# Halved operands for the low-rank products, head sums and centering of a time-mixing layer

## The chip, the cores and the metric

The kernel runs on one core of a Trainium2 chip. The metric is the device time of one execution in microseconds. Times of several runs are given as their median. The profile is of one execution of its own.

## What is computed

One inference step of a two-layer decoder trunk, a prompt of 512 tokens and 8 sample sequences of 8 tokens sharing the weights (576 columns in the kernel). Layer 0 mixes over time (RWKV-7), layer 1 uses windowed attention; each layer has two gated feed-forward blocks. Only the mixing of layer 0 is touched by the change:

```python
w_log = -softplus(-(w0 + tanh(xw @ w1) @ w2)) - 0.5
decay = exp(-exp(w_log))
a = sigmoid(a0 + (xa @ a1) @ a2)            # low rank, 64
g = sigmoid(xg @ g1) @ g2                   # low rank, 160
kk = k * k_k;  kk = kk / max(sqrt(sum(kk*kk, per head)), 1e-12)
k = k * (1 + (a - 1) * k_a);  b = kk * a
# per token: S = S*w + (S @ -kk) b^T + v k^T;  y = S r
y = (y - mean(y, per head)) * rsqrt(var + eps) * lnx_w + lnx_b
y = y + sum(r * k * r_k, per head) * v
return (y * g) @ w_o
```

## The kernel before

Everything is kept with features on the partitions: 1024 features are 8 tiles of 128, and one such tile, two heads, is called a pair (p = 0 to 7). A product over the 576 columns is made in two halves of 288 (`halves`).

**Dense products.** The large weights come in fp32 and are split: `load_w` (line 166) loads 512 columns on SP's queue, ACT copies them to a rounded type (`H`, line 177) and POOL subtracts to get the rest (`L`, line 178). The activations are split the same way by `split` (line 160). A product then is three passes, `WH XH + WH XL + WL XH` (line 697). Smaller products, among them the ones of the change, are plain fp32 matmuls.

**The stage.** The phase "r" (line 1719) loads constants (`rwkv_consts`, line 1678): `bo` sums over the 64 rows of a head, `cen` subtracts the mean of a head. `rwkv` (line 631) makes the mixed inputs, the low-rank activations `tw`, `ta` (rows 0 to 63 for the rate a, rows 64 to 95 for the last 32 rows of the gate) and `sg` (lines 653 to 670). Then it weaves five streams of work (line 823):

- `keys` and `inverses` for each pair: decay, normalised key (`kk`, line 864, with a head sum on line 868), rate a (line 881), the scaled keys B and K (lines 914 to 917), and the inverse of a small triangular matrix on DVE with two trips through DRAM (lines 948 to 962). The keys of pair p wait for the chain of pair p-4.
- `scores` for each pair, after the chain of pair p-2: products between keys and queries, a Neumann series, then the bonus sum (line 1068, whose input `y` is written on line 1063 into one of two buffers, so the post step of pair p-2 has to be through), transposes.
- `chain` for each pair, one after the other: 8 chunks, each a short round of PE and DVE.
- `decode` and `post` for each pair: the centering (line 1197), the variance (line 1207), the gate (lines 1220 and 1221) and a split of the result. The last pair has its own version, `post_last`.
- the dense products: key, receptance and value projections, then the output projection in parts.

**Order.** `weave` (line 578) is a planner: it runs the streams against a clock of its own, which each product advances by its expected length (line 567), always takes the stream that is ready first, and lets the dense stream in at a limited rate, more when few columns were planned lately. A stream's `yield 0.9` is a pause of 0.9 us on that clock, in which other streams' work is placed. A scheduler below it orders each engine's instructions by this sequence and by when buffers come free. Each engine then executes its queue in order.

Of the kernel before, what the change touches and what calls it, by code (L numbers as in the profile page):

```python
# [9 lines left out]
F32R = mybir.dt.float32r  # L10
# [45 lines left out]
N_P = 5  # L56
# [36 lines left out]
class Body:  # L93
# [537 lines left out]
    def rwkv(self, done, wi):  # L631
        nc, I, O = self.nc, self.I, self.O
# [7 lines left out]
        for k in range(DT):  # L640
            n = self.ht(k, "n")
            nc.vector.scalar_tensor_tensor(n, self.h[k], self.vec("n01", k), rs, op0=ALU.mult, op1=ALU.mult)
            x = self.ht(k, "h")
# [9 lines left out]
        tw = self.s("tw")  # L653
# [9 lines left out]
        self.dense(I["w1"], K8, xm, lambda hf, ps, sl: self.act(tw[0:64, sl], ps, AF.Tanh), nw=64, outer=True)  # L663
        ta = self.s("ta")
        self.dense(I["a1"], K8, self.mixed("ma", "AR", M_A), lambda hf, ps, sl: nc.scalar.copy(ta[0:64, sl], ps), nw=64, outer=True)
        sg = self.s("sg")
        xg = self.mixed("mg", "AR", M_A)
        self.dense(I["g1a"], K8, xg, lambda hf, ps, sl: self.act(sg[:, sl], ps, AF.Sigmoid), outer=True)
        self.dense(I["g1b"], K8, xg, lambda hf, ps, sl: self.act(ta[64:96, sl], ps, AF.Sigmoid), nw=32, outer=True)
        self.tw, self.ta, self.sg = tw, ta, sg  # L670

# [151 lines left out]
        self.weave([chain_gen(), score_gen(), rest_gen(), key_gen(), dense_gen(seq)], R_LS, R_RATE, R_WARM)  # L823

    def keys(self, p, V):

        nc, I, c_ = self.nc, self.I, self.rc
# [3 lines left out]
        A, R = V["AR"][:, 0], V["AR"][:, 1]  # L831
# [10 lines left out]
        lw2 = self.s("l1", cols=128)[0:65]  # L842
        la2 = self.s("l2", cols=128)[0:64]
        for t, n in ((lw2, "w2"), (la2, "a2")):
            nc.sync.dma_start(t, I[n][p])
        st = self.s("p1", N_P, cols=512)
# [17 lines left out]
        kk = self.s("p1", N_P)  # L864
        nc.scalar.activation(kk, k, AF.Square, scale=self.vec("kk", p))
        for sl in halves:
            ps = self.bank("w", HF)
            self.mm(ps, c_["bo"], kk[:, sl], start=True, stop=True)
            nc.vector.tensor_scalar(kk[:, sl], ps, 1e-24, None, op0=ALU.max)
            yield 0.9  # L870
            self.mark(f"kk{p}")
# [6 lines left out]
        a = self.s("p1", N_P)  # L878
        for sl in halves:
            ps = self.bank("w", HF)  # L880
            self.mm(ps, la2, self.ta[0:64, sl], start=True, stop=True)
            self.act(a[:, sl], ps, AF.Exp, scale=-1.0, bias=self.na0[:, p:p + 1])
            yield 0.9
            self.mark(f"a{p}")
# [87 lines left out]
    def scores(self, p, V):  # L972
# [91 lines left out]
        bkc = BK[:, 0:NC].rearrange("p c z t -> p c (z t)")  # L1064
        nc.vector.tensor_tensor(bkc, bkc, V["pcc"].to_broadcast([128, NC, 128]), op=ALU.mult)
        for sl in halves:
            ps = self.bank("i", HF)
            self.mm(ps, c_["bo"], y[:, sl], start=True, stop=True)
            nc.vector.tensor_tensor(v[:, sl], ps, v[:, sl], op=ALU.mult)
            yield 0.5  # L1070
            self.mark(f"neu{p}")
# [113 lines left out]
    def post(self, p, V, z):  # L1185
# [3 lines left out]
        self.mark(f"post{p}")  # L1189
        lg2 = self.s("l3", cols=128)  # L1190
        lg3 = self.s("l4", cols=128)
        for t, n in ((lg2, "g2a"), (lg3[64:96], "g2b")):
            nc.sync.dma_start(t, I[n][p])
        yc, s2 = V["y"], V["s2"]
        for sl in halves:
            ps = self.bank("q", HF)
            self.mm(ps, c_["cen"], yc[:, sl], start=True, stop=True)
            nc.scalar.copy(yc[:, sl], ps)
            yield 0.8
            self.mark(f"post{p}")  # L1200
# [17 lines left out]
        for sl in halves:  # L1218
            ps = self.bank("q", HF)
            self.mm(ps, lg2, self.sg[:, sl], start=True, stop=False)  # L1220
            self.mm(ps, lg3[64:96], self.ta[64:96, sl], start=False, stop=True)
            nc.vector.tensor_tensor(zt[:, sl], ps, yc[:, sl], op=ALU.mult)
            yield 0.8
            self.mark(f"post{p}")
# [4 lines left out]
    def post_last(self, p, V, z):  # L1229
# [3 lines left out]
        self.mark(f"post{p}")  # L1233
        lg2 = self.s("l3", cols=128)
        lg3 = self.s("l4", cols=128)
        for t, n in ((lg2, "g2a"), (lg3[64:96], "g2b")):
            nc.sync.dma_start(t, I[n][p])
        yc, rd, bv = V["y"], V["s2"], V["bv"]
        gt, gw = self.s("vo", N_VO), self.s("vo", N_VO)
        for sl in halves:  # L1240
            ps = self.bank("q", HF)
            self.mm(ps, lg2, self.sg[:, sl], start=True, stop=False)
            self.mm(ps, lg3[64:96], self.ta[64:96, sl], start=False, stop=True)
            nc.scalar.copy(gt[:, sl], ps)
            nc.gpsimd.tensor_scalar(gw[:, sl], gt[:, sl], self.vec("lw", p), None, op0=ALU.mult)
            nc.vector.scalar_tensor_tensor(gt[:, sl], bv[:, sl], self.vec("lb", p), gt[:, sl], op0=ALU.add, op1=ALU.mult)
            yield 0.8
            self.mark(f"post{p}")
# [429 lines left out]
    def rwkv_consts(self):  # L1678
        nc = self.nc
        self.rc = {}  # L1680
        for n in ("tri", "triS", "bo", "cen", "id", "bm", "mb", "md", "mq"):
            self.rc[n] = self.const(n, self.ph)
        self.leps = self.ph.tile([128, 1], F32, name="leps")
        nc.vector.memset(self.leps, LNX_EPS)
# [173 lines left out]
```

## Time and profile before

| | us |
|---|---|
| median of 3 runs (2851.83 to 2859.78) | 2859.17 |
| the profiled execution, its own time | 2855.7 |
| its span, first to last instruction | 2853.9 |

Busy shares of the span: PE 95% (2723.6 us), its weight loads 89%, DVE 55%, POOL 54%, ACT 45%. The mean granted clock of TensorE is 0.981 of full speed.

How to read the profile: PE is the matrix engine (PEld its weight loads, which run beside it), DVE the vector engine, ACT the scalar engine, POOL the general one, SP the queue that issues loads. `ps_w<-p,bo` is a product into the PSUM tile ps_w from the tiles p and bo. An fp32 product stands as two records. The records' ends are modelled, so what a product holds PE for is read from one start to the next. A name such as `p` or `l` stands for all tiles of that name with a number behind it.

### The profile page before, as it was taken

To read this page: it belongs to the slowest core of one execution; us is meant where nothing else is said; L and a number is where in the kernel's file an instruction comes from. 1 tells how busy PE (TensorE), PEld (TensorE's weight loads), DVE (VectorE), ACT (ScalarE), POOL (GpSimd) and SP (SyncE) were. 2 spreads that over 40 slices of the span, in tenths; PEclk is the share of its full clock that TensorE was granted. 3 is DMA by queue.
4 is the path that set the end of the run, shared out by engine and by line. 5 is a ranking of instruction groups with operands and counts; after the bars stand their busy time and mean duration, and the time that the engine had idled before them with its cause. 6 is when DMAs were issued, how large, how long until landed. Compare 5 with 4: busy or idle time off the path is not lost.

```text
span 2853.9 us, 56130 instructions
## 1 busy us (share of the span) xinstructions
PE 2723.6 (95%) x21952; PEld 2540.3 (89%) x21952; DVE 1560.1 (55%) x3258; ACT 1297.2 (45%) x2548; POOL 1528.6 (54%) x1256
## 2 busy tenths in 40 slices
PE   8999997998999999999999999999999999999997
PEld 7999996986767778999999999999888878999997
DVE  6543529557677756633436554243577776533435
ACT  4443535434333225434545444353555655443544
POOL 5665748554243335756753466574544325766753
PEclk9999998999999999999999999999999999999999
DMA  4232234222112112232333222324334443232323
GB/s 134 83 96 85 85 97 151 67 69 57 53 40 80 41 47 84 78 97 86 98 92 103 93 82 93 91 80 125 108 85 104 141 141 115 79 92 86 93 86 96
DMA packets 177085, 257.80 MB, mean 90 GB/s; under 512 B 46889, under 2 KB 70897, under 8 KB 176820
## 3 DMA queue, kind: packets, MB, share of 16 engines
q1 hardware_dynamic: 148736, 223.56, 26.1%
q10 hardware_dynamic: 28084, 30.66, 4.1%
q8 instruction: 172, 2.82, 0.4%
q14 instruction: 93, 0.76, 0.1%
HBM read 234.31 MB, written 19.85 MB: 89 GB/s over the span
## 4 chain that ended last, share of the span: by engine, by line
PE 51%; DVE 6%; ACT 2%; issue 1%; DMA 1%; POOL 0%; DVEq 0%; ACTq 0%; POOLq 0%
PE ps_e L204 23%; PE ps_e L409 15%; PE ps_d L561 5%; PE ps_d L409 2%; PE ps_s L561 2%; PE ps_o L561 1%; DVE S L1357 1%; PE ps_pt L570 1%; DVE ps_q L351 1%; DVE S L1352 1%; DMA D<-rev 1%; DVE x L321 0%; ACT sh L343 0%; ACT QS L1426 0%; ACT wh L177 0%
## 5 line engine op out<-in xcount | busy, mean ns | idle before, releaser
L178 POOL TENSOR_TENSOR wl<-wr,wh 128x512 fp32r<-128x512 f32 (+2 forms) x477 | 604.9, 1277 | 728.1 <-ACT wh L177 687.8
L204 PE MATMUL ps_e<-hv,wh 128*128 128x288 f32 x2944 | 588.6, 295 | 2.5 <-POOL hv L163 1.3
L177 ACT CAST wh<-wr 128x512 fp32r<-128x512 f32 (+2 forms) x477 | 277.2, 587 | 546.4 <-PE ps_e L204 293.2
L204 PEld LDWEIGHTS ps_e<-hv,wh 128*128 128x128 f32 x2944 | 473.4, 188 | 3.8 <-POOL hv L163 2.2
L204 PE MATMUL ps_e<-hv,wl 128*128 128x288 f32 x1472 | 434.8, 296 | 1.2 <-POOL wl L178 1.2
L561 PE MATMUL ps_d<-x,wh 128*128 128x288 f32 x1664 | 369.1, 309 | 6.2 <-ACT wh L177 2.2
L204 PE MATMUL ps_e<-x,wh 128*128 128x288 f32 x1792 | 362.6, 297 | 10.6 <-ACT x L269 7.4
L204 PEld LDWEIGHTS ps_e<-x,wh 128*128 128x128 f32 x1792 | 289.5, 189 | 12.6 <-ACT x L269 7.4
L561 PEld LDWEIGHTS ps_d<-x,wh 128*128 128x128 f32 x1664 | 274.4, 191 | 26.6 <-issue 9.3
L204 PEld LDWEIGHTS ps_e<-hv,wl 128*128 128x128 f32 x1472 | 276.9, 188 | 1.5 <-POOL wl L178 1.4
L466 DVE SCALAR_TENSOR_TENSOR h<-ps_e,h 128x288 f32<-128x288 f32 x192 | 87.7, 457 | 335.0 <-PE ps_e L204 335.0
L204 PE MATMUL ps_e<-x,wl 128*128 128x288 f32 x896 | 264.5, 296 | 0.0
L561 PE MATMUL ps_d<-x,wl 128*128 128x288 f32 x832 | 250.2, 301 | 0.3 <-POOL wl L178 0.3
L409 PE MATMUL ps_e<-x,wh 128*128 128x288 f32 x1056 | 213.2, 295 | 0.0
L346 POOL TENSOR_TENSOR wl<-wr,wh 128x512 fp32r<-128x512 f32 x136 | 197.2, 1454 | 18.3 <-ACT wh L343 12.6
L409 PE MATMUL ps_e<-TH,wh 128*128 128x288 f32 x544 | 163.3, 300 | 9.8 <-DVE t L383 6.9
L409 PEld LDWEIGHTS ps_e<-x,wh 128*128 128x128 f32 x1056 | 169.1, 188 | 3.9 <-issue 3.9
L204 PEld LDWEIGHTS ps_e<-x,wl 128*128 128x128 f32 x896 | 169.0, 189 | 0.2
L409 PE MATMUL ps_e<-TH,wl 128*128 128x288 f32 x544 | 161.4, 297 | 0.0
L561 PEld LDWEIGHTS ps_d<-x,wl 128*128 128x128 f32 x832 | 159.1, 191 | 2.2 <-issue 0.5
L409 PE MATMUL ps_e<-TL,wh 128*128 128x288 f32 x544 | 160.9, 296 | 0.0
L409 PE MATMUL ps_e<-x,wl 128*128 128x288 f32 x528 | 155.1, 295 | 0.0
(402 smaller groups left out, 6395.4 us busy)
## 6 DMA issues: line engine op xcount, KB each, us to landing
wr<-in_f1wi SPq DMA_DIRECT2D x108, 256.0 KB
wr<-in_f2wi SPq DMA_DIRECT2D x108, 256.0 KB
sr<-in_f1wi SPq DMA_DIRECT2D x68, 256.0 KB
sr<-in_f2wi SPq DMA_DIRECT2D x68, 256.0 KB
wr<-in_f1wo SPq DMA_DIRECT2D x64, 256.0 KB
wr<-in_f2wo SPq DMA_DIRECT2D x64, 256.0 KB
wr<-in_wrkv SPq DMA_DIRECT2D x48, 256.0 KB
wr<-in_wq SPq DMA_DIRECT2D x48, 256.0 KB
```

Source lines behind the costliest of these rows:

```text
L177: nc.scalar.copy(H, raw)
L178: nc.gpsimd.tensor_tensor(L, raw, H.bitcast(F32), op=ALU.subtract)
L204: nc.tensor.matmul(ps[0:nw], a, b[:, sl], start=k + m == 0, stop=3 * k + m == n - 1)
L346: eng.tensor_tensor(L, a, H.bitcast(F32), op=ALU.subtract)
L351: i = nc.vector.tensor_tensor(t, a, b, op=op).ins
L409: nc.tensor.matmul(ps, a, b, start=first and k + m == 0, stop=k == DT // 2 - 1 and m == 2, skip_group_check=True)
L466: nc.vector.scalar_tensor_tensor(h[:, sl], ps, 0.5, h[:, sl], op0=ALU.mult, op1=ALU.add)
L561: self.nc.tensor.matmul(out, lhsT, rhs, **kw)
L570: self.nc.tensor.transpose(out, in_, ident)
L1352: nc.vector.tensor_tensor_reduce(dst, ps, bias, -1.0, 3.0e38 if mx is None else mx, op0=ALU.add, op1=ALU.min, accum_out=m)
L1357: nc.vector.tensor_tensor(S[:, a], S[:, a], S[:, b], op=ALU.add)
```

## The change

The head sums of the squared key (line 868) and of the bonus product (line 1068) and the centering (line 1197, pairs 0 to 6) no longer use fp32 operands. Their moving operand is split into two rounded halves (`halves_of`: ACT copies, POOL subtracts, two buffers H shared by the three users), and the product is two passes against a rounded constant (`mm2`). The rate product (line 881) and the two gate products (lines 1220, 1221 and in `post_last`) are made of three passes (`mm3`); their weights are split after loading (`small`, ACT and POOL), and `ta` and `sg` are split once, ahead of the pairs. The first three get a pause of 2.5 us in the planner after the split. The centering of the last pair, the variance sums and the decay products stay fp32. In `rwkv`, `ta` and `sg` now lie in the ring `p1` until they are split into tiles of their own.

```diff
@@ rwkv
-        ta = self.s("ta")
+        ta = self.s("p1", N_P)
...
-        sg = self.s("sg")
+        sg = self.s("p1", N_P)
...
-        self.tw, self.ta, self.sg = tw, ta, sg
+        self.tw = tw
+        self.ta, self.sg = self.dbl("taR", 1, F32R), self.dbl("sgR", 1, F32R)
+        for a, b in ((slice(0, 64), nc.vector), (slice(64, 96), nc.gpsimd)):
+            self.split(ta[a], self.ta[a, 0], self.ta[a, 1], b)
+        self.split(sg, self.sg[:, 0], self.sg[:, 1])
@@ new functions
+    def small(self, ap, tag, rows):
+        t = self.s(tag, cols=128)
+        HL = self.ph.tile([128, 2, 128], F32R, name=tag + "R", tag=tag + "R", bufs=1)
+        self.nc.sync.dma_start(t[rows], ap)
+        return self.split(t[rows], HL[rows, 0], HL[rows, 1], self.nc.gpsimd)
+
+    def mm3(self, ps, W, X, sl, rows=slice(0, 128), first=True, last=True):
+        (WH, WL), (XH, XL) = W, (X[rows, 0, sl], X[rows, 1, sl])
+        for m, (a, b) in enumerate(((WH, XH), (WH, XL), (WL, XH))):
+            self.mm(ps, a, b, start=first and m == 0, stop=last and m == 2)
+
+    def mm2(self, ps, c, X, sl):
+        for i in range(2):
+            self.mm(ps, c, X[i][:, sl], start=i == 0, stop=i == 1)
+
+    def halves_of(self, x):
+        return self.split(x, self.s("H", 2, F32R), self.s("H", 2, F32R), self.nc.gpsimd)
@@ keys
-        la2 = self.s("l2", cols=128)[0:64]
+        la2 = self.small(I["a2"][p], "l2", slice(0, 64))
...
+        sq = self.halves_of(kk)
+        yield 2.5
...
-            self.mm(ps, c_["bo"], kk[:, sl], start=True, stop=True)
+            self.mm2(ps, self.boR, sq, sl)
...
-            self.mm(ps, la2, self.ta[0:64, sl], start=True, stop=True)
+            self.mm3(ps, la2, self.ta, sl, slice(0, 64))
@@ scores
+        yR = self.halves_of(y)
+        yield 2.5
...
-            self.mm(ps, c_["bo"], y[:, sl], start=True, stop=True)
+            self.mm2(ps, self.boR, yR, sl)
@@ post
-        lg2 = self.s("l3", cols=128)
-        lg3 = self.s("l4", cols=128)
...
+        lg2 = self.small(I["g2a"][p], "l3", slice(0, 128))
+        lg3 = self.small(I["g2b"][p], "l4", slice(64, 96))
+        yR = self.halves_of(yc)
+        yield 2.5
...
-            self.mm(ps, c_["cen"], yc[:, sl], start=True, stop=True)
+            self.mm2(ps, self.cenR, yR, sl)
...
@@ post and post_last
-            self.mm(ps, lg2, self.sg[:, sl], start=True, stop=False)
-            self.mm(ps, lg3[64:96], self.ta[64:96, sl], start=False, stop=True)
+            self.mm3(ps, lg2, self.sg, sl, last=False)
+            self.mm3(ps, lg3, self.ta, sl, slice(64, 96), first=False)
@@ rwkv_consts
+        self.boR, self.cenR = (self.ph.tile([128, 128], F32R, name=n + "R") for n in ("bo", "cen"))
+        nc.scalar.copy(self.boR, self.rc["bo"])
+        nc.scalar.copy(self.cenR, self.rc["cen"])
```

## Rows read from the trace of the kernel before

**Rows 1.** busy time by stretch of the time mixing; columns in its first line

```profile
core 0: us, PE busy (x) PEld busy (x) DVE busy (x) ACT busy (x) POOL busy (x), PEclk, DMA share, GB/s
511.00:592.00 81.00, 79.11 (x571) 75.46 (x569) 32.28 (x27) 38.79 (x76) 44.88 (x34) 1.00 0.22 70
592.00:690.00 98.00, 80.84 (x599) 70.99 (x597) 73.32 (x133) 39.50 (x86) 48.04 (x37) 0.91 0.26 68
690.00:890.00 200.00, 190.49 (x2246) 142.53 (x2245) 134.96 (x394) 72.78 (x172) 60.73 (x54) 0.95 0.19 52
890.00:1085.00 195.00, 189.70 (x2042) 136.75 (x2039) 135.81 (x384) 62.62 (x152) 71.33 (x72) 0.97 0.19 50
```

**Rows 2.** who PE waited for, 580 to 1105 us: total us, times, longest

```profile
PE ps_w L561 <- DVE BK L915: 13.7, 10, 4.6
```

**Rows 3.** busy time and clock in stretches of 10 us, same columns

```profile
660.00:670.00 10.00, 6.03 (x43) 5.50 (x42) 8.11 (x14) 3.71 (x9) 7.73 (x8) 1.00 0.57 143
670.00:680.00 10.00, 8.15 (x65) 7.23 (x66) 7.13 (x8) 1.88 (x6) 4.10 (x3) 0.66 0.17 58
```

**Rows 4.** timeline of PE around a head-sum product: start us, length us, instruction, count

```profile
579.88 0.65 PE L561 MATMUL ps_w<-p,bo 128*128 128x288 f32 x2
580.15 0.64 PE L561 MATMUL ps_d<-x,wh 128*128 128x288 f32 x2
580.63 0.29 PE L561 MATMUL ps_d<-x,wl 128*128 128x288 f32 x1
```

**Rows 5.** the chain that ended last, a stretch of dense products

```profile
1206.47 44.50 PE ps_e L204 x336
```

**Rows 6.** the changed products: ns min/median/max, first and last start, shape

```profile
L561 PE MATMUL ps_w<-p,bo x32: 403/406/511, 579.9 to 931.9; 128*128 128x288 f32 x32
L561 PE MATMUL ps_q<-y,cen x32: 403/406/847, 747.6 to 1080.5; 128*128 128x288 f32 x32
L561 PE MATMUL ps_w<-ta,l x32: 402/455/507, 583.3 to 941.8; 64*128 64x288 f32 x32
```

**Rows 7.** POOL's groups by form, 592 to 1085 us: busy us, mean ns

```profile
L163 POOL TENSOR_TENSOR AR<-y,AR 128x576 fp32r<-128x576 f32 x7 | 9.9, 1409 | 28.4 <-ACT AR L162 17.8 <-DMA dN<-iv 5.7 <-DMA l<-in_g2b 2.5
L178 POOL TENSOR_TENSOR wl<-wr,wh 128x256 fp32r<-128x256 f32 x24 | 19.6, 817 | 59.1 <-ACT wh L177 51.4 <-issue 6.7 <-PE ps_y L561 0.8
```

**Rows 8.** ACT's groups by form, 592 to 1085 us, same columns

```profile
L162 ACT CAST AR<-y 128x576 fp32r<-128x576 f32 x7 | 4.7, 672 | 23.8 <-DVE y L1222 17.7 <-DMA dN<-iv 6.1
```

**Rows 9.** two DVE lines: ns min/median/max, first and last start

```profile
L913 DVE TENSOR_TENSOR p<-p,p x8: 745/1930/2036, 594.0 to 951.6; 128x576 f32<-128x576 f32 x8
L959 DVE TENSOR_TENSOR iv<-iv x112: 159/197/1397, 611.5 to 985.2; 72x14 f32<-72x14 f32 x16, 72x26 f32<-72x26 f32 x16, 72x36 f32<-72x36 f32 x16, 72x44 f32<-72x44 f32 x16
```

**Rows 10.** timeline of POOL at the seam before the key projections

```profile
508.97 7.16 POOL L163 TENSOR_TENSOR x<-AR,x 128x576 fp32r<-128x576 f32 x4 [0.41 <-ACT x L162]
```

**Rows 11.** timeline of PE around a rate product over 64 rows

```profile
583.33 0.75 PE L561 MATMUL ps_w<-ta,l 64*128 64x288 f32 x2
584.00 0.54 PE L561 MATMUL ps_d<-x,wh 128*128 128x288 f32 x2
584.38 0.29 PE L561 MATMUL ps_d<-x,wl 128*128 128x288 f32 x1
```

**Rows 12.** timeline of PE at the gate of pair 0

```profile
770.06 0.75 PE L561 MATMUL ps_q<-sg,l 128*128 128x288 f32 x2
...
770.75 0.34 PE L561 MATMUL ps_x<-n,BK 128*64 128x64 f32 x4
...
771.13 0.75 PE L561 MATMUL ps_q<-ta,l 32*128 32x288 f32 x2
```

**Rows 13.** POOL's and DVE's timeline at pair 2; the chains' ends

```profile
779.06 1.41 POOL L163 TENSOR_TENSOR AR<-y,AR 128x576 fp32r<-128x576 f32 x1 [7.67 <-ACT AR L162]
780.50 1.65 DVE L1063 SCALAR_TENSOR_TENSOR y<-AR,vecs,BK 64x576 f32<-64x576 f32 x2 [0.57 <-POOL AR L163]
L1180 ACTq DMA_DIRECT2D out_wkvp<-Z x8: 338/344/368, 747.5 to 1079.6; - x8
```

More of the change, by code (lines that the diff above doesn't have):

```diff
@@ L842, in keys @@
         lw2 = self.s("l1", cols=128)[0:65]
-        la2 = self.s("l2", cols=128)[0:64]
-        for t, n in ((lw2, "w2"), (la2, "a2")):
-            nc.sync.dma_start(t, I[n][p])
+        nc.sync.dma_start(lw2, I["w2"][p])
+        la2 = self.small(I["a2"][p], "l2", slice(0, 64))
         st = self.s("p1", N_P, cols=512)
@@ L865, in keys @@
         nc.scalar.activation(kk, k, AF.Square, scale=self.vec("kk", p))
+        sq = self.halves_of(kk)
+        yield 2.5
+        self.mark(f"kk{p}")
         for sl in halves:
             ps = self.bank("w", HF)
-            self.mm(ps, c_["bo"], kk[:, sl], start=True, stop=True)
+            self.mm2(ps, self.boR, sq, sl)
             nc.vector.tensor_scalar(kk[:, sl], ps, 1e-24, None, op0=ALU.max)
@@ L1065, in scores @@
         nc.vector.tensor_tensor(bkc, bkc, V["pcc"].to_broadcast([128, NC, 128]), op=ALU.mult)
+        yR = self.halves_of(y)
+        yield 2.5
+        self.mark(f"neu{p}")
         for sl in halves:
             ps = self.bank("i", HF)
-            self.mm(ps, c_["bo"], y[:, sl], start=True, stop=True)
+            self.mm2(ps, self.boR, yR, sl)
             nc.vector.tensor_tensor(v[:, sl], ps, v[:, sl], op=ALU.mult)
@@ L1189, in post @@
         self.mark(f"post{p}")
-        lg2 = self.s("l3", cols=128)
-        lg3 = self.s("l4", cols=128)
-        for t, n in ((lg2, "g2a"), (lg3[64:96], "g2b")):
-            nc.sync.dma_start(t, I[n][p])
+        lg2 = self.small(I["g2a"][p], "l3", slice(0, 128))
+        lg3 = self.small(I["g2b"][p], "l4", slice(64, 96))
         yc, s2 = V["y"], V["s2"]
+        yR = self.halves_of(yc)
+        yield 2.5
+        self.mark(f"post{p}")
         for sl in halves:
             ps = self.bank("q", HF)
-            self.mm(ps, c_["cen"], yc[:, sl], start=True, stop=True)
+            self.mm2(ps, self.cenR, yR, sl)
             nc.scalar.copy(yc[:, sl], ps)
@@ L1233, in post_last @@
         self.mark(f"post{p}")
[L1234 to L1237, printed above, removed]
+        lg2 = self.small(I["g2a"][p], "l3", slice(0, 128))
+        lg3 = self.small(I["g2b"][p], "l4", slice(64, 96))
         yc, rd, bv = V["y"], V["s2"], V["bv"]
@@ L1241, in post_last @@
             ps = self.bank("q", HF)
-            self.mm(ps, lg2, self.sg[:, sl], start=True, stop=False)
-            self.mm(ps, lg3[64:96], self.ta[64:96, sl], start=False, stop=True)
+            self.mm3(ps, lg2, self.sg, sl, last=False)
+            self.mm3(ps, lg3, self.ta, sl, slice(64, 96), first=False)
             nc.scalar.copy(gt[:, sl], ps)
```

## The prediction, made before the change was run

> **What bounds the kernel now.** The page comes first: PE is busy 95% of the span. The chain of work that ended last reaches back only to 1106 us, where the time mixing is over, so it says nothing of the stage that this change touches; that stage has to be read from the busy time by stretch [rows 1]. The time mixing runs from about 511 to 1105 us. From 592 to 1085 us, in the three later stretches, PE is busy 80.84 + 190.49 + 189.70 = 461 of 493 us, DVE 344, POOL 180, ACT 175. The reader is to see that PE has 32 us of idle time there (6.5%), and that no other engine is above three quarters in any of these stretches. PE executes in its order, with the dense projections as filler between short bursts of the recurrence, so a product that gets shorter lets all that is queued behind it start sooner. I read this stage as bound by PE's queue, with two weak places. One is the wait of PE for the scaled keys that DVE writes on line 915, the largest single wait that PE has on another engine, 13.7 us in ten pieces [rows 2]. The other is PE's clock: of the 50 stretches of 10 us from 592 us on, ten have a mean granted clock below 1.00, one of the deepest 0.66 [rows 3], so part of those ran at 1.2 GHz instead of 2.4 GHz. Added up the ten lack 2.39 stretches of full clock, 24 us of work at the full level. That row also shows what came before the fall: PE busy in only 8.15 of 10 us, with the row before it at 6.03.
>
> **The change part by part.** *The products.* An fp32 product of 288 columns stands in the trace as two records. Among dense products it can be priced exactly [rows 4]: from the start of the head-sum product at 579.88 to the start of the third dense record after it at 580.63 lie 0.75 us. The two dense products in between take what a stream of such products takes, 44.50 us for 336, 0.1325 us each [rows 5]. So the fp32 product holds PE for 0.75 - 0.265 = 0.485 us, and the same product as one pass over each half takes 0.1325 us a pass.
> Head sums and centering become two passes: 0.485 - 0.265 = 0.22 us less. There are 16 head sums of squared keys and 16 of the bonus product (32 records of either kind, two to a product [rows 6]). Of the 16 centering products those of the last pair stay fp32, so 14 change. 46 x 0.22 = 10.1 us. The constants are exact in rounded form, so they need no second half.
> The low-rank products become three passes, 0.485 - 0.3975 = 0.0875 us less: 16 for the rate a and 32 for the gate (16 with g2a, 16 with g2b [rows 6]), 48 x 0.0875 = 4.2 us. Together PE loses 14.3 us of queue. Because 6.5% of its time there is idle anyway, I count 93.5% of it: 13.4 us.
> *The splits.* Each halving is a copy on ACT and a subtraction on POOL. A 128x576 subtraction into the same kind of tile takes 1.41 us on POOL [rows 7] and the copy 0.67 us on ACT [rows 8]. There are 8 for the squared keys, 8 for the bonus product, 7 for the centering: 23, so 32.4 us of POOL and 15.4 us of ACT. The small weights (a2, g2a, g2b of 8 pairs: 24 tiles of 128 columns) have no row of their own shape. The nearest on POOL has 256 columns, 0.82 us [rows 7]; nothing and the whole of that bound them, and I take half, 0.41, 9.8 us in all. On ACT the 0.67 us of the large copy is the upper bound; I take 0.3, 7 us in all. POOL goes from 180 to 222 of 493 us, ACT from 175 to 198. Neither becomes the bound by its sum, so this costs nothing by itself. What covers it is the dense filler on PE; without the cover each of the 23 halvings would stand on the path with 0.67 + 1.41 = 2.1 us, 48 us in all.
> *POOL beside DVE.* The DVE product on line 913 takes 0.745 us at best, but 1.93 us in the median [rows 9], in a stretch in which POOL runs lines 902 and 917; a DVE operation with two SBUF inputs is about 1.1 us longer when POOL is at work. If PE's wait for line 915 grows with POOL's busy time, by 42/180 = 23%, it adds 13.7 x 0.23 = 3.2 us. Bounds: nothing (the halvings fall elsewhere) and 23 x 1.1 = 25 us (each meets such an operation ahead of a PE wait). I take 3, since the only row that shows what PE loses to it is [rows 2].
> *The seam.* The activations ta and sg are now split once, where the key mixing is prepared: three ACT copies of at most 0.67 us, a POOL subtraction of 1.4 us at most and two on DVE. There POOL runs 7.16 us without a gap [rows 10], and PE, busy 79.11 of 81 us after 511 [rows 1], consumes what they make. Bounds 0 and 4 us (POOL's 1.41 and a DVE subtraction at its long form, twice 1.3); I take 1, because these splits are needed only by the first rate product at 583 us and can slip in behind.
> *Queues and order.* The small weights load on SP's queue as before and in the same places. What is new is that ACT and POOL wait for them instead of PE. Their buffers come free once the previous pair has read them, a pair's length ahead of the next use, so I cost that at nothing; a late one would hold ACT's queue, with the evacuations of the dense products behind it. The three users of the two buffers H queue behind one another: a centering and the head sum of a new key pair start after the same chain. The planner also sees three new pauses of 2.5 us and shorter products, so the order changes everywhere.
> *The sum.* 13.4 - 3 - 1 = 9.4 us less. Against the profiled execution, 2855.7 us (its span is 2853.9): 2846.3. The median of the runs is 3.5 us above that execution, so in its terms 2859.2 - 9.4 = 2849.8, say 2850. This case alone reaches from 2844 (all 14.3 us and no cost) to 2857.
>
> **A rule against it.** A product over 64 rows costs more than its passes: from 583.33 the next product of another shape starts only at 584.00, and two dense products then take 0.38 instead of 0.27 us [rows 11]. So a change of tile shape costs some 0.19 us before and 0.11 after. The Trainium skill says as much ("TensorEngine Tiling (Array Packing)", Key Properties): changing the tiling mode drains the engine. By that rule the passes of one product should stay together, and three are easier to tear apart than two records: the two gate products, written one after the other, already have a chain product of a third shape between them [rows 12].
>
> **The rivals.** *The wait takes the gain (chance 0.15).* The bonus product of pair p is written into the buffer of y of pair p-2, and POOL's last subtraction of that pair ends at 780.47, and DVE, idle for 0.57 us on it, starts line 1063 at 780.50 [rows 13]. So the path from the end of chain p-2 through the post step to scores p and chain p is tight at places, and gets two halvings longer, 5 us a round by the pauses, three rounds: 15 us. For it: that idle time. Against: chains end 47.4 us apart (332.1 us for seven [rows 13]), 95 us a round, of which the pauses written in the code for a chain, a post step and the end of scores are some 35. With half the rounds bound, 7.5 us come in and half of 13.4 goes: +1, about 2860.
> *DVE and POOL collide (0.20), the slower side.* Place: lines 902 to 917, and line 959 of the inverses, while a halving of another pair runs on POOL. Price 1.1 us each [rows 9], 25 us for all 23; it turns the sign from about 11 of 23 on (12 us of gain left after the seam). Full: 25 + 1 - 13.4 = +12.6, so 2872. For it: line 913 is at its long form in the median. Against: POOL is idle 55% of the time even afterwards, and line 959, 112 times, is short in the median, 0.197 against 1.397 us at most [rows 9]. The Trainium skill ("SBUF — State Buffer", SBUF: two separate sides) states this as a rule: the port pair that the two engines share is locked by whichever starts first, for its whole instruction. The row agrees with it, 1.93 against 0.745 us.
> *Fewer falls of the clock (0.14).* The same work in less time leaves PE fewer gaps. If a third of the 24 us lost to 1.2 GHz goes, 8 us join the 9.4: 2842. The reverse is within the slower rival.
> *It doesn't do what it says (0.05).* If each of the 48 three-pass products is torn apart once, 48 x 0.19 = 9 us go back: 2859.
>
> **How the numbers follow.** A measurement of this kernel tells a change from none at about 0.3%, 8.6 us, so faster means below 2850.6. The forecast has 0.46; it straddles that line, 0.28 faster and 0.18 same. The waiting rival: 0.13 same, 0.02 slower. The collisions: 0.18 slower, 0.02 same. The clock: 0.14 faster. Torn products: 0.05 same. Together 0.42, 0.38, 0.20. For 8 in 10 the range goes down to 2838, a little below the clock case, and up to 2870, short of the full collision.
>
> **What would show it.** The fp32 records of the head sums and of the low-rank products are gone, and a head sum holds PE 0.27 us; else the first term is wrong. PE's busy time between 592 us and the end of the last chain falls by about 13 us and its idle time stays near 32; if the idle time grows by as much, the waiting rival holds. Line 913 and PE's wait for line 915 tell the collisions: if the wait stays below 17 us, that term was right. The count of stretches below full clock tells the third rival. The prediction is wrong if the stage's length changes by more than PE's own work, above all if chains start later after the one before them.

## The result, and the profile after

The change made the kernel slower: 2883.37 us median against 2859.17, a ratio of 1.0084 (95% interval 1.0069 to 1.0100). The forecast was 2850 with a range of 2838 to 2870; the time lies outside it, on the other side of no change. The profiled execution took 2882.47 us; its span is 2880.4.

Busy time by stretch after (columns as in [rows 1]: the stretch and its length; busy time and instructions of PE, of its weight loads, of DVE, ACT and POOL; granted clock; DMA share; GB/s):

```profile
511.00:592.00 81.00, 79.10 (x579) 75.91 (x577) 36.61 (x26) 39.86 (x77) 50.42 (x35) 1.00 0.23 73
592.00:690.00 98.00, 83.25 (x560) 75.52 (x558) 71.04 (x117) 40.11 (x88) 53.83 (x44) 0.81 0.24 66
690.00:890.00 200.00, 185.32 (x2201) 144.07 (x2201) 140.21 (x387) 81.13 (x193) 77.83 (x72) 0.95 0.16 42
890.00:1085.00 195.00, 182.21 (x2009) 136.47 (x2007) 131.36 (x371) 65.47 (x160) 81.34 (x82) 0.94 0.19 52
```

The seam up to 592 us is as before. Then PE's clock is lower: 0.81 for 0.91 in the second line, 0.94 for 0.97 in the last, and PE's idle time from 592 to 1085 us is 42 us instead of 32. All eight chains end late, by 4 to 23 us and not steadily more: the first by 13.3 us, the fifth by 4.4, the last by 22.6 (first and last start of the DMA that ends a chain, [rows 13] before: 747.5 to 1079.6):

```profile
L1209 ACTq DMA_DIRECT2D out_wkvp<-Z x8: 338/344/368, 760.8 to 1102.2; - x8
```

A new head sum is as short as reckoned. On PE's timeline one among dense products (start, length, form) holds PE from 584.99 to 585.25:

```profile
584.99 0.43 PE L561 MATMUL ps_w<-H,boR 128*128 128x288 f32 x2
585.25 0.43 PE L561 MATMUL ps_d<-x,wh 128*128 128x288 f32 x2
```

What PE waited for from 590 to 1110 us (us in all, times, longest), and how POOL's queue stood:

```profile
PE ps_w L561 <- DVE BK L941: 10.5, 7, 3.7
PE ps_i L561 <- POOL H L163: 10.4, 7, 5.2
PE ps_q L561 <- POOL H L163: 2.6, 3, 1.8
...
POOL H L163 <- ACT H L162: 43.3, 10, 12.6
```

The first line answers to [rows 2] and has not grown. The next two are new: the bonus sum and the centering reach the head of PE's queue before their operand is halved. In the last line POOL stands 43 us in front of subtractions whose first half ACT has not yet copied. Such a stand is no loss by itself: of the 520 us from 590 to 1110 POOL is idle for 322 before the change and for 294 after it.

**A measure for what follows.** Over the 52 stretches of 10 us from 590 to 1110 us I add up one less the granted clock ("lost at the clock", in us at full clock), and beside it PE's idle time. Before it is 24.0 and 35.5 us, after 41.0 and 43.7: together 25.2 us more, and the span is 26.5 longer. As far as this sum goes the time is in these two, and two thirds of it is PE at 1.2 GHz instead of 2.4.

### The profile page after: what moved, and what is told of

The parts are those of the page before. It is cut to its first block, busy times and chain, and to the rows that moved or that the text cites. A ratio compares the mean times of both kernels' runs of the same rounds, so it can differ in the third digit from the quotient of the medians.

```text
span 2880.4 us, 56352 instructions
## 1 busy us (share of the span) xinstructions
PE 2733.9 (95%) x22000; PEld 2562.1 (89%) x22000; DVE 1578.9 (55%) x3260; ACT 1317.5 (46%) x2600; POOL 1579.0 (55%) x1304
## 3 DMA queue, kind: packets, MB, share of 16 engines
q1 hardware_dynamic: 148736, 223.56, 25.6%
## 4 chain that ended last, share of the span: by engine, by line
PE 56%; DVE 6%; ACT 3%; issue 2%; POOL 2%; DMA 1%; DVEq 0%; ACTq 0%; SPq 0%; POOLq 0%
PE ps_e L204 23%; PE ps_e L409 15%; PE ps_d L561 7%; PE ps_d L409 2%; PE ps_s L561 2%; PE ps_q L561 1%; PE ps_o L561 1%; PE ps_i L561 1%; PE ps_pt L570 1%; DVE ps_q L351 1%; PE ps_x L561 1%; DVE S L1385 1%; DVE S L1380 1%; ACT wh L177 0%; DVE x L321 0%
## 5 line engine op out<-in xcount | busy, mean ns | idle before, releaser
L346 POOL TENSOR_TENSOR wl<-wr,wh 128x512 fp32r<-128x512 f32 x136 | 196.4, 1448 | 18.6 <-ACT wh L343 12.5
```

The costliest lines, as they stand in the source:

```text
L346: eng.tensor_tensor(L, a, H.bitcast(F32), op=ALU.subtract)
```

## The experiments

All numbers in one table. Median and ratio to the kernel before, run beside it; the other columns are of the profiled execution.

| | what it is | median us | ratio, 95% interval | span | clock lost | PE idle | last chain end |
|---|---|---|---|---|---|---|---|
| before | | 2859.2 | | 2853.9 | 24.0 | 35.5 | 1079.6 |
| after | the change | 2883.4 | 1.0084 (1.0069 to 1.0100) | 2880.4 | 41.0 | 43.7 | 1102.2 |
| e1 | low-rank part alone | 2891.5 | 1.0115 (1.0100 to 1.0130) | 2905.3 | 70.0 | 39.5 | 1122.2 |
| e2 | centering alone | 2862.8 | 1.0022 (1.0012 to 1.0032) | 2857.5 | 25.5 | 39.0 | 1080.5 |
| e3 | squared keys alone | 2880.0 | 1.0080 (1.0068 to 1.0093) | 2879.8 | 51.0 | 37.3 | 1108.6 |
| e4 | bonus sum alone | 2861.4 | 1.0017 (1.0008 to 1.0026) | 2861.4 | 25.6 | 38.0 | 1079.5 |
| e5 | e1, old booking | 2855.1 | 0.9984 (0.9972 to 0.9997) | 2860.4 | 32.4 | 30.6 | 1086.4 |
| e6 | before, booking of e1 | 2870.2 | 1.0037 (1.0024 to 1.0051) | 2866.8 | 40.8 | 35.2 | 1087.8 |
| e7 | change, old booking, no pauses | 2906.6 | 1.0159 (1.0134 to 1.0185) | 2904.8 | 83.6 | 39.5 | 1131.3 |
| e8 | before, pause and booking of e3 | 2877.8 | 1.0066 (1.0041 to 1.0092) | 2874.5 | 51.1 | 36.3 | 1104.5 |
| e9 | e7, extra passes | 2896.9 | 1.0131 (1.0104 to 1.0157) | 2896.7 | 47.6 | 37.8 | 1120.1 |
| e10 | change, extra passes | 2891.9 | 1.0114 (1.0088 to 1.0141) | 2889.6 | 39.2 | 44.6 | 1114.5 |
| e11 | change, old booking | 2907.3 | 1.0176 (1.0134 to 1.0219) | 2897.5 | 61.3 | 43.5 | 1114.9 |
| e12 | e11 without the squared keys | 2877.2 | 1.0070 (1.0041 to 1.0099) | 2875.4 | 32.3 | 41.4 | 1096.5 |
| e13 | e7, no subtraction | 2865.6 | 1.0026 (1.0015 to 1.0038) | 2865.6 | 34.0 | 35.8 | 1089.0 |
| e14 | change, no subtraction | 2858.2 | 1.0001 (0.9980 to 1.0022) | 2866.9 | 44.3 | 36.9 | 1092.4 |
| e15 | before, halvings unread | 2887.6 | 1.0102 (1.0080 to 1.0124) | 2882.3 | 42.7 | 40.3 | 1107.6 |
| e16 | before, one pause | 2878.2 | 1.0060 (1.0045 to 1.0075) | 2877.7 | 42.6 | 34.3 | 1103.7 |
| e17 | before, POOL's load alone | 2856.9 | 0.9986 (0.9974 to 0.9998) | 2851.9 | 27.3 | 33.3 | 1080.1 |
| e18 | change, subtraction on DVE | 2897.4 | 1.0123 (1.0096 to 1.0150) | 2890.6 | 59.8 | 35.9 | 1112.9 |

In the 17 kernels without extra passes other than before, the sum of the two middle columns moves by 1 to 64 us and the span by -2 to 51, never more than 13 us apart, so the sum tells large differences only. The profiled execution can be far from the median: that of e1 took 2907.1 us, that of e14 2868.7, that of e5 2862.1. The ten executions of e14 reach from 2851.7 to 2875.9 us, and of the ten of e16 nine lie between 2876.6 and 2879.5 and one at 2864.0.

**The parts alone (e1 to e4).** Each keeps one part of the change and puts the old lines back for the others: e1 only `mm3` with `small` and the split of `ta` and `sg`; e2 only the centering; e3 only the squared keys; e4 only the bonus product. As an example, what e4 keeps of the change in `scores`:

```diff
+        yR = self.halves_of(y)
+        yield 2.5
+        self.mark(f"neu{p}")
         for sl in halves:
             ps = self.bank("i", HF)
-            self.mm(ps, c_["bo"], y[:, sl], start=True, stop=True)
+            self.mm2(ps, self.boR, yR, sl)
```

> Only the rate and gate products are changed (three passes, small weights and ta, sg split); head sums and centering stay fp32 without halvings and pauses. If the loss is PE waiting for halvings (theory W), this part waits for none late and wins its 4 us of PE queue less the seam: 2 to 4 us faster than before. If POOL's added work slows DVE (theory C), its 24 small and 3 seam splits cost about 3 us: 0 to 3 slower. If any new order costs (theory P), it is some 5 to 10 us slower although its products are shorter.

> Only the centering of pairs 0 to 6 is changed (7 halvings, 7 pauses of 2.5 us, 14 products of two passes). W: PE waited 2.6 us for these halvings in the changed kernel against 3 us of shorter products: within 4 us of before. C: 7 of 23 halvings, a third of the loss: 7 us slower. P: not to be told in advance, 0 to 10 us slower.

> Only the head sum of the squared keys is changed (8 halvings, 8 pauses, 16 products of two passes). W: PE waited 0.3 us directly for these halvings, so 3 us faster to 3 us slower, unless the keys that come later make PE wait more for line 915. C: a third of the loss, 8 us slower. If the falls of the clock between 592 and 690 us come from the later keys of pairs 0 to 3, this part alone shows the mean clock of about 0.81 there and is some 10 us slower.

> Only the head sum of the bonus product is changed (8 halvings, 8 pauses, 16 products of two passes). W: PE waited 12 us for these halvings in the changed kernel, the longest time 5.2 us with a fall of the clock behind it, against 3.5 us of shorter products: 8 to 15 us slower, most of the loss. C: a third of the loss, 8 us slower. P: anything from 0 to 10 us slower.

The part with the least work on POOL, e1, is the worst (+33 us by its ratio), and the parts add up to +67 us where the whole has +24. So no sum of prices holds; none of the three theories had the 33 us of e1 or the 23 of e3. The bonus part costs 5 us alone, but alone it lacks the wait that it has in the change: PE waits 0.3 us in front of this sum for the subtraction, not 10.4. So e4 does not price that wait.

How long POOL stood in front of its subtractions and PE in front of this sum in e4, and then POOL in e3 (590 to 1110 us):

```profile
POOL H L163 <- ACT H L162: 18.9, 6, 5.6
...
PE ps_i L561 <- POOL H L163: 0.3, 1, 0.3
```

```profile
POOL H L163 <- ACT H L162: 42.3, 6, 19.9
```

The time of e1 is in stretches in which PE is busy throughout at 1.2 GHz, where the kernel before has a clock of 1.00:

```profile
830.00:840.00 10.00, 10.00 (x89) 8.04 (x89) 5.81 (x18) 1.88 (x4) 2.31 (x3) 0.50 0.03 10
840.00:850.00 10.00, 10.00 (x85) 7.82 (x84) 3.38 (x11) 1.52 (x5) 2.31 (x3) 0.50 0.33 74
```

**Booking (e5, e6).** `mm` books each pass in the planner's clock and column list, so three short passes are booked as three quarters of the time and 1.5 times the columns of the fp32 product, and the filler is placed otherwise. e5 is e1 with the old booking, e6 the kernel before with that of e1.

```diff
 # e5, in mm3; mm2 likewise
-            self.mm(ps, a, b, start=first and m == 0, stop=last and m == 2)
+            self.nc.tensor.matmul(ps, a, b, start=first and m == 0, stop=last and m == 2)
+        self.cols.append((self.clk, HF * WH.shape[0] / 128 * 2))
+        self.clk += 4 * HF / 2400
 # e6, for the rate and gate products; told() issues the fp32 product and books it n times
-            self.mm(ps, la2, self.ta[0:64, sl], start=True, stop=True)
+            self.told(3, ps, la2, self.ta[0:64, sl], start=True, stop=True)
```

> Low-rank products in three passes as in e1, but each product is booked in the planner's clock and column list as the fp32 product it replaces, so PE gets the order of the kernel before. Order theory (e1 lost its 33 us because the planner, told 1.5 times the columns in a quarter of the time per pass, lets less dense filler in between the chains and PE's clock falls): about 2853 us (2847 to 2860), clock loss in the stage near the 24 us of before. If the products, the splits or the seam themselves are the cause (halvings, tile-shape changes, shared buffers p1): it stays at 2880 to 2893.

> The kernel before, fp32 products, no split anywhere; only the planner is told for each of the 48 low-rank products what three passes would be (order of e1 with the old work). Order theory: as slow as e1 or a little slower, 2885 to 2900 us, with the dense filler between first and last chain end thinned as in e1 (415 products against 457) and the clock loss at 50 us or more. If the work itself is the cause: 2857, no change.

With the old booking the low-rank part loses nothing and may gain (ratio 0.9984, the 4.2 us of the sum would be 0.9985). Its splits, the small weights behind ACT and POOL and the seam therefore cost nothing that shows. The booking alone costs the kernel before 11 us, a third of e1's loss, not all of it as the order theory had it: the shorter products and the other order lose more together than either alone. The order of e6 is near that of e1, not the same: of some 4450 records of PE from 592 to 1100 us, the changed products left out, 480 stand elsewhere (the records outside the longest sequence that both traces share; the counts below are made in the same way).

**The whole with the old booking, and the pause (e7, e8, e16).** e7 books as e5 and takes out the three pauses. e8 and e16 leave the fp32 products alone:

```diff
 # e16: this line alone; e8 also books the head sum as two passes
         nc.scalar.activation(kk, k, AF.Square, scale=self.vec("kk", p))
+        yield 2.5
+        self.mark(f"kk{p}")
```

> The whole change, with each product booked as the fp32 one and without the three pauses, so that the order is almost that of the kernel before. Order theory: the gain of the shorter products shows, 2846 us (2838 to 2856). Rival, waits on the halvings: PE now meets the sums before ACT and POOL have halved the operands, 23 times up to 2 us, 2860 to 2885. Collision rival: 2872.

> The kernel before, fp32 products, no halving; the planner is told two passes for each of the 16 head sums of squared keys and has the 2.5 us pause in keys (order of e3 with the old work). Order theory: near e3, 2872 to 2888 us, first chain end late (760 us) and the clock below 0.88 from 592 to 690 us. If the halvings themselves cost e3 its 23 us: 2857 to 2862.

> The kernel before with one line more, the pause of 2.5 us ahead of the head sum of squared keys; fp32 products, old booking, no halving. With e8 (2877.8, pause and new booking) it parts the pause from the booking. If the pause is what moves the order: 2870 to 2880. If the booking is: 2857 to 2863.

e16 differs from the kernel before in no operation, only in when the planner places the head sum of the squared keys. In order it is no small change: some 1700 of PE's 4800 records stand elsewhere, as many as in the change itself. It loses 17 us by its ratio, e8 19, and e3 with the real halvings 23: most of that part's loss is the order which the pause makes. PE idles no longer than before (34.3 against 35.5 us); of the 23.8 us by which the span grows, 18.6 are lost at the clock. Its stretches from 670 us:

```profile
670.00:680.00 10.00, 5.58 (x44) 4.78 (x45) 6.90 (x9) 2.44 (x7) 4.50 (x3) 0.55 0.30 58
680.00:690.00 10.00, 10.00 (x62) 8.08 (x62) 6.60 (x13) 1.13 (x3) 1.27 (x1) 0.50 0.32 93
690.00:700.00 10.00, 10.00 (x88) 8.46 (x87) 1.21 (x4) 4.01 (x9) 0.00 (x0) 0.59 0.04 12
```

After one poor stretch PE is busy throughout and still at 1.2 GHz. e7 refutes the simple order theory: placed nearer to the kernel before (some 650 of 4800 records elsewhere, against 1660 in the change), the change is slower still, with the largest loss at the clock of all.

**Extra passes (e9, e10).** Ahead of each new product passes are written into the same bank and overwritten, until it has four again: 140 passes of 0.1325 us [rows 5], 18.6 us more for PE.

```diff
     def mm2(self, ps, c, X, sl):
+        for _ in range(2):
+            self.nc.tensor.matmul(ps, c, X[0][:, sl], start=True, stop=True)
 ...
```

> e7 (2906.6 us) with extra passes written into the same bank ahead of each new product, unbooked, and overwritten: every head sum, centering and low-rank product has four passes again, about 19 us more work for PE at full clock, halvings and order unchanged. Clock theory (the shortened products are missing as work between the gaps, so that PE falls to 1.2 GHz and stays there): clock loss falls from 84 us to 20 to 45 and the time, although PE does more, to 2860 to 2885. Wait theory (PE waits on the halvings, the clock follows from that idle time): the loss stays above 65 us and the time at 2905 to 2925.

> The change as it is with the same unbooked extra passes, in its own order. Clock theory with order: part of the 41 us of clock loss goes, part is the order's: about 2870 to 2885 although PE has 19 us more work. If shortness has nothing to do with the clock: 2883 + 13 to 19, so 2896 to 2902.

e9 has 18.6 us more work than e7 and takes no longer (8 us less by the ratios, whose intervals overlap); the loss at the clock falls from 83.6 to 47.6 us. The same stretch in e7, and then in e9:

```profile
830.00:840.00 10.00, 10.00 (x90) 8.11 (x89) 4.99 (x21) 2.52 (x8) 2.32 (x3) 0.50 0.04 10
840.00:850.00 10.00, 10.00 (x97) 7.86 (x97) 3.59 (x10) 2.32 (x5) 3.44 (x3) 0.50 0.20 29
850.00:860.00 10.00, 10.00 (x58) 6.60 (x58) 4.63 (x11) 0.50 (x1) 0.00 (x0) 0.50 0.01 2
```

```profile
830.00:840.00 10.00, 9.44 (x137) 8.03 (x135) 9.37 (x34) 3.15 (x9) 3.23 (x4) 1.00 0.17 50
840.00:850.00 10.00, 9.35 (x154) 7.85 (x155) 8.76 (x25) 3.15 (x6) 3.42 (x3) 1.00 0.21 31
850.00:860.00 10.00, 10.00 (x96) 6.93 (x95) 3.50 (x11) 4.91 (x11) 1.85 (x4) 1.00 0.09 31
```

Time and loss lie between the ranges written for the two theories, so the clock theory holds at best in part. In the change's own order (e10) the loss hardly moves and the time grows by 9 us. So the added work goes with less time at 1.2 GHz in one order and not in the other. It also moved other records: some 520 of PE's in e9 against e7, 510 in e10 against the change. That the missing work made the clock fall is therefore not shown.

**Pauses or booking in the whole (e11, e12).** e11 is the change with the old booking and its pauses; e12 also leaves the squared keys as before.

> The change with its three pauses, each product booked as the fp32 one: tells the pauses from the missing pauses of e7. If the pauses are what keeps PE from meeting unfinished halvings, 2860 to 2880, below e7's 2907; if they do nothing, 2895 to 2910. The clock loss tracks it in either case: time less 2830 within 12 us of the loss.

> The change without the squared-keys part, old booking, two pauses: the parts that cost least alone (+6, +4.5) with the one that gained in the old order (e5, -4). If the parts were additive: 2859 + 6 + 4.5 - 4 = 2865, less what the old booking gives back. Clock theory: anything from 2848 (loss as in before, all of 10.8 us gained) to 2880, and time less 2830 tracks the loss.

e11 equals e7, so the pauses are not what protects PE there, and the old booking makes the change 26 us slower where it made the low-rank part 37 us faster (by the ratios). No order here is good for every kernel. e12 costs 20 us, where the parts that it keeps cost 6, 5 and -5 us by themselves (e2, e4, e5): they do not add up here either.

**The subtraction (e13, e14).** Each of the 22 halvings in this stretch (one more is earlier) is left with ACT's copy; both passes read it and the second overwrites the first, so the low halves are missing from the sums. The edit does one thing more: a halving now takes one of the two buffers H and not both, so the next one need not wait until PE has read the last.

```diff
     def halves_of(self, x):
-        return self.split(x, self.s("H", 2, F32R), self.s("H", 2, F32R), self.nc.gpsimd)
+        H = self.s("H", 2, F32R)
+        self.nc.scalar.copy(H, x)
+        return H, H
```

> e7 (2906.6 us; whole change in the old order, no pauses) without POOL's subtraction: each of the 23 big halvings is ACT's copy alone, and both passes read that copy (the low halves are left out of the sums). PE's work, order and ACT's work are those of e7; 32 us of POOL and the second half of each halving's latency are gone. If the latency of the halvings starts the falls of the clock: 2845 to 2865, clock loss back to 20 to 40. If the missing work of the shortened products starts them: 2885 to 2910, loss above 60.

> The change as it is, with its pauses and its own order, without POOL's 23 big subtractions (both passes read ACT's copy, the low halves are left out). PE's waits for POOL's H (13 us) go. If the latency of the halvings is what costs: 2845 to 2862. If order and shortness cost: 2866 to 2884 (only the 13 us of waits, or less, come back).

The change without POOL's subtractions takes 2858 us: by the ratios 24 us come back, all of its loss (the interval of e14 is 6 us to either side). In e7 it is 38 us, down to 2866. PE's own waits for POOL's H are 13 us in the change. The forecast gain of 9 us does not appear even so. What hangs on the subtraction is more than one thing, and these runs take it all away at once: PE's waits, the buffers (POOL's wait for PE, 6.6 us in a group line further below), whatever stands behind the subtraction in POOL's queue, and the order, because the scheduler places the rest anew: some 400 of PE's records stand elsewhere in e14 than in the change, 190 in e13 than in e7.

**The halvings as load (e15, e17).** The kernel before, with the halvings beside its fp32 products and no product reading them (e15), and then POOL's operation alone, with no copy of ACT ahead of it (e17).

```diff
 # e15, after the square of the keys; likewise for y after the bonus product and for yc in post
+        self.halves_of(kk)
 # e17, halves_of
-        return self.split(x, self.s("H", 2, F32R), self.s("H", 2, F32R), self.nc.gpsimd)
+        self.nc.gpsimd.tensor_tensor(self.s("H", 2, F32R), x, x, op=ALU.subtract)
```

> The kernel before with its fp32 products, booking and order, and the 23 big halvings on ACT and POOL issued beside them, which no product reads. Prices the halvings as load on the two engines alone (collisions of POOL with DVE, places in ACT's queue, the buffers held). If the load alone costs: 2870 or more. If only what waits for the halvings costs: 2856 to 2864.

> e15 without ACT's copies: the kernel before, and beside it 23 unread subtractions of 128x576 on POOL alone (x - x), in POOL's queue behind what makes x, but behind no copy of ACT. e15 cost 29 us. If POOL's busy time and its sharing with DVE cost it: 2878 to 2890 again. If POOL's queue stands still because a subtraction waits there for a copy that is itself queued on ACT (51 us in 11 pieces in e15's trace), or if the copies on ACT cost: 2856 to 2868.

Unread halvings cost 29 us. POOL's operations alone cost nothing: 2856.9 us, with PE's instructions in the order of the kernel before (some 15 of 4800 records differ). In e15 some 250 stand elsewhere. The timelines around the halving of one key pair show the difference. First the kernel before, then e17, then e15: the square of the keys on ACT, the line that overwrites it in place with the head sum (DVE, L869 and L873), POOL's splits of the dense operand and the line that PE waits for in [rows 2] (start, length, operation; in brackets the idle time before it and its releaser):

```profile
642.01 0.77 ACT L865 ACTIVATE p<-AR,vecs 128x576 f32<-128x576 f32 x1
...
645.51 6.13 POOL L163 TENSOR_TENSOR x<-n,x 128x576 fp32r<-128x576 f32 x4 [10.26 <-ACT x L162]
646.34 0.46 DVE L869 TENSOR_SCALAR p<-ps_w 128x288 f32<-128x288 f32 x1 [0.77 <-PE ps_w L561]
...
667.90 3.26 POOL L917 TENSOR_TENSOR BK<-p,p 64x576 f32<-64x576 f32 x2
670.01 3.50 DVE L915 TENSOR_TENSOR BK<-p,p 64x576 f32<-64x576 f32 x2
```

```profile
641.86 0.77 ACT L868 ACTIVATE p<-AR,vecs 128x576 f32<-128x576 f32 x1
...
642.71 1.15 POOL L826 TENSOR_TENSOR H<-p 128x576 fp32r<-128x576 f32 x1 [7.46 <-ACT p L868]
...
645.55 6.14 POOL L163 TENSOR_TENSOR x<-n,x 128x576 fp32r<-128x576 f32 x4 [1.69 <-ACT x L162]
646.26 0.46 DVE L873 TENSOR_SCALAR p<-ps_w 128x288 f32<-128x288 f32 x1 [0.65 <-PE ps_w L561]
...
667.91 3.26 POOL L921 TENSOR_TENSOR BK<-p,p 64x576 f32<-64x576 f32 x2
670.02 3.52 DVE L919 TENSOR_TENSOR BK<-p,p 64x576 f32<-64x576 f32 x2
```

```profile
644.12 0.77 ACT L868 ACTIVATE p<-AR,vecs 128x576 f32<-128x576 f32 x1
...
647.88 0.66 ACT L162 CAST H<-p 128x576 fp32r<-128x576 f32 x1
...
648.62 1.42 POOL L163 TENSOR_TENSOR H<-p,H 128x576 fp32r<-128x576 f32 x1 [12.20 <-ACT H L162]
...
650.00 6.25 POOL L163 TENSOR_TENSOR x<-n,x 128x576 fp32r<-128x576 f32 x4
...
651.39 0.44 DVE L873 TENSOR_SCALAR p<-ps_w 128x288 f32<-128x288 f32 x1
...
672.91 3.26 POOL L921 TENSOR_TENSOR BK<-p,p 64x576 f32<-64x576 f32 x2
675.02 3.52 DVE L919 TENSOR_TENSOR BK<-p,p 64x576 f32<-64x576 f32 x2
```

In e17 the halving slips into a gap, and the lines behind it start within 0.08 us of their old times. In e15 POOL stands 12.2 us in front of the subtraction, but in the kernel before it stands 10.3 us in front of the splits at the same place. Of the 4.5 us by which these splits are late, 2.1 us were there already at the square of the keys; the copy on ACT and the subtraction came on top. The scaled keys are 5.0 us late, as is the line that overwrites the squared keys (651.39 for 646.34). In e15 all eight first-half lines of this kind wait for a semaphore of POOL, since the subtraction still reads what they overwrite; in the kernel before one of the eight does. So halvings that no product reads are waited for all the same. The centering, whose result overwrites its operand too, shows it (590 to 1110 us, in e15), below what POOL stood in front of its subtractions over the stage:

```profile
POOL H L163 <- ACT H L162: 51.0, 11, 12.2
...
ACT y L1204 <- POOL H L163: 6.4, 3, 3.5
```

The subtraction is through 1.2 us after the square in e17 and 5.2 us after it in e15, behind ACT's copy. So subtractions without copies cost nothing (e17), copies without subtractions leave the change at the time of the kernel before (e14), and the two one behind the other cost 24 to 38 us with all that follows from them. Which of the things that follow makes the time is not shown. POOL's stand is no measure of it: 18.9 us in e4, which costs 5, and 42.3 us in e3, which costs little more than its order alone (e16). e17 also leaves the second buffer H free, as e13 and e14 do, and every slow kernel with halvings takes both.

**On DVE (e18).** The change, the subtraction on DVE (no engine named in `split`).

> The change as it is, its order and pauses, with the 23 big subtractions on DVE in place of POOL. e14, without them, took 2858. If it is POOL's queue that makes the change slow: 2855 to 2868, although DVE gets 17 to 32 us more. If any engine that has to do them loses the time (latency before the sums, DVE on the path): 2872 to 2895.

It is 11 us slower than the change by the ratios, whose intervals just overlap, and far from the 2855 to 2868 expected if POOL's queue were what makes the change slow. DVE does not stand in front of the halvings (1.4 us in all), and the subtractions are short; the loss at the clock is 59.8 us. Some 440 of PE's records stand elsewhere than in the change.

```profile
DVE H L163 <- ACT H L162: 1.4, 3, 0.6
...
L163 DVE TENSOR_TENSOR H<-y,H 128x576 fp32r<-128x576 f32 x15 | 15.5, 1034 | 0.9 <-ACT H L162 0.8
```

So moving the subtraction off POOL is no remedy, POOL's queue alone does not explain the loss, and what e18 lost by is not settled. No kernel here beats both the kernel before and the change by more than a measurement can tell; nearest are e5, the low-rank part with the old booking, at 0.9984, and e17 at 0.9986, which does nothing useful more.

## Why the prediction was wrong

**What held.** A head sum holds PE 0.26 us (0.27 forecast). POOL's halving takes 1.42 to 1.49 us in the mean and ACT's 0.67, and the small ones, estimated at 0.41 and 0.3, measured 0.46 to 0.51 and 0.30 (groups of POOL and ACT, 580 to 1110 us: busy us, mean ns, idle before and its releasers):

```profile
L163 POOL TENSOR_TENSOR H<-y,H 128x576 fp32r<-128x576 f32 x15 | 22.3, 1490 | 20.8 <-ACT H L162 20.5
L163 POOL TENSOR_TENSOR H<-p,H 128x576 fp32r<-128x576 f32 x7 | 10.0, 1422 | 37.8 <-ACT H L162 22.8 <-issue 7.9 <-PE ps_i L561 6.6
L163 POOL TENSOR_TENSOR l2R<-l,l2R 64x128 fp32r<-64x128 f32 x7 | 3.6, 510 | 14.3 <-ACT l2R L162 14.2
L162 ACT CAST l3R<-l 128x128 fp32r<-128x128 f32 x7 | 2.1, 298 | 25.2 <-PE ps_q L561 25.1
```

The seam costs nothing that shows (forecast 1). The wait for the scaled keys did not grow (10.5 us after, 13.7 before; 3 more were forecast).

**The step that failed: "Neither becomes the bound by its sum, so this costs nothing by itself."** The splits were priced by the busy share of POOL and ACT. POOL's busy time does cost nothing, as e17 shows. But a halving is a copy in ACT's queue and then a subtraction that waits for it, and more waits for the end of that pair than the sum which reads it. With the big subtractions gone the change is 24 us faster (e14), another order of it 38 us (e13); beside the old products the halvings cost the kernel before 29 us (e15). The prediction has nothing where these stand. How they come about stays open: PE's waits (13 us in the change), in-place overwrites, the buffers H, POOL's queue and the order were not parted, and e18 speaks against POOL's queue as the whole of it. The prediction had the pieces, a late small weight that holds ACT's queue and three users of two buffers H, and gave none of them a price; for the small weights e5 shows no loss. Its remark that without cover the halvings would cost 48 us asked only whether PE has work while the operand is halved.

**A step left without a price: "the order changes everywhere".** One pause, with every operation as before, costs 17 us (e16), one booking 11 us (e6). In the other direction, e5 and e1 differ by 37 us through the booking alone. The term needed bounds of some 20 us; with them the sign of a 9 us gain could not be told.

**The rivals.** *DVE and POOL collide* had the right sign and nearly the right time (2872) for a wrong reason. The line that should have shown it, 1930 ns in the median before [rows 9], has not grown in the change (min/median/max):

```profile
L939 DVE TENSOR_TENSOR p<-p,p x8: 759/1892/1984, 598.6 to 969.4; 128x576 f32<-128x576 f32 x8
```

The rule of the Trainium skill weighed there ("SBUF — State Buffer", SBUF: two separate sides) is not contradicted, but in e17 it moved no end: that kernel has 23 more POOL operations and the time of before. *The wait takes the gain*: the wait is there, 10.4 us in front of the bonus sum, and what it costs was not measured: e4, which costs 5 us, has 0.3 us of it, and e14 takes it away together with the rest. *Fewer falls of the clock* went the other way, 24 to 41 us, and "the reverse is within the slower rival" gave it no mechanism and no price, though it carries two thirds of the loss. *Torn products*: the low-rank part with the old booking loses nothing (e5), so it has no weight there.

**The gain of 14 us** of PE's work cannot be seen in the total. Span less clock loss less idle time is 2794 us before and 2796 after, 2782 in e7, 2787 in e8 with the old work: a scatter as large as the term. Only the median of e5 agrees with its share. In the prediction's first case the ends are loose: 2859.2 - 14.3 is 2844.9, not 2844, and 2857 has no working. And [rows 6], cited for the gate, shows the rate products only.

**What stays open.** Why the clock falls deeper, and what it is in an order that makes it good or bad, was not settled; e16 and e6 only show the size. ACT's copies were not tried alone in the kernel before, nor the change with buffers H enough for two halvings, nor any halving kernel with PE's order held. So the 24, 29 and 38 us are those of the subtractions with the order that they bring, and not of POOL's queue.

## To carry to other kernels

Do not price an operation made of two engines' work in sequence by busy shares. List what waits for its second half: the product that reads it, a line that overwrites its operand in place, the buffers that it holds, what stands behind it in the queue. Where a planner places the work, changing what it is told (a pause, a booked length) is a change of its own: run it alone with the old work before crediting or blaming the new. And where PE's clock is below 1.00 in many stretches, a change of order needs a price of its own, from the loss that is there already.

## What was not expected of the hardware

PE can stay at 1.2 GHz while it is busy throughout: three stretches of 10.00 busy us at 0.50 in e7. Adding 18.6 us of useless passes did not make that kernel slower (e9). Twenty-three further operations on POOL beside DVE cost nothing (e17), while a reordering of the same operations cost 17 us (e16).
